# Transposes of the second half moved into the up projection, pools shared with the down projection, and other operand forms in the norms

## The chip, the cores and the metric

The kernel runs on one core of one Trainium2 chip. Its time is the device time of one execution in microseconds (us). A core has five engines, each with its own queue of instructions that it works through in order: PE (TensorE, matmuls, into PSUM), DVE (VectorE), ACT (ScalarE), POOL (GpSimd) and SP (SyncE, which here issues all DMAs). A difference of under about 0.2% (5 us) can't be told from none.

## The reference

One layer of a decoder: 2048 rows of 1024, all float32.

```python
proj = x @ w_in                       # columns: q, k, v, B, C, h, p
mix = concat(stick_breaking_attention(q, k, v), short_conv(B, C, h), multiscale_pool(p))
mix = head_group_rmsnorm(mix, mix_norm_g) @ w_o
x = layer_norm(ALPHA * x + mix, ln1_g, ln1_b)
hid = square(relu(x @ w_up))          # 4096 columns
x = layer_norm(ALPHA * x + hid @ w_down, ln2_g, ln2_b)
```

## The kernel before

Every float32 operand of a matmul is split into a high part (an ACT copy to the float32r type) and a low part (a subtraction on DVE or GpSimd), and three products (high by high, high by low, low by high) stand for one. The rows are worked on in four chunks of 512 (`c`), each of four tiles of 128 (`t`).

`phase1` has four stages, whose instructions a scheduler interleaves when the program is built: the input projections, the attention (which sets the pace of DVE), the output product with the first norm (`out_stage`), and the up projection (`Up`). A tile of rows leaves `out_stage` as `r`: PE adds up 24 products for each of two halves of 512 columns in one of two PSUM banks (`dense_ps`), DVE adds the residual (L549) and does the norm (L87 to L110), and `r` goes to memory (`x1scr`). Two products later `transposed` turns the tile: four PE transposes (128 by 128) to a bank, and from the banks seven operands `B11, T2, B21, T3, T1, T4, B22`, sums and differences of quarters for a Strassen-Winograd scheme with seven products in place of eight. `put` splits each (ACT L571, then DVE or GpSimd L572) and stores both parts in `tscr`, by way of four staging buffers.

The up projection runs over two halves of 1024 rows (chunks 0 and 1, then 2 and 3). In each, 16 `quad`s make four tiles of hidden values with seven products of 12 matmuls from the seven operands `x` (2 MB each, loaded from `tscr`) and seven weights `w` made by `weights`. The first three `x` stand in pool `upx`, the next two in `upm`, the last two and the hidden tiles `h` in `upr`. These pools take over memory of the earlier stages: `upm` that of `xw` and `mixw` (operands of the output product), `upr` that of `mixw` and `dense` (tiles `r`, staging buffers, raw loads). A tile waits until the tiles that lay there are done with. `h` goes to memory (`hscr`).

`down` opens new pools when `phase1` has closed its own. In eight groups `g` of 512 hidden columns it loads four rows of tiles of `w_down` (`draw`, split into `dh`, `dl`) and hidden values (`hr`, split into `hh`, `hl`), and makes 32 sums of 12 matmuls; DVE adds each to `y` (L832 in the first group, L834 after). In the last group each of the 16 row tiles, once complete, gets the second norm: statistics, an inverse root by ACT and three small DVE instructions (L100 to L102), the scaling on ACT (L847), the product with `ln2_g` on DVE (L848), the sum with `ln2_b` on GpSimd (L849). The last tile has a shorter path on DVE alone (L842, L843).

Of the kernel before, what the change touches and what calls it, by code (L numbers as in the profile page):

```python
# [40 lines left out]
EARLY, LATE = 4, 8  # L41


def build(nc, tc, ctx, A, out):
# [50 lines left out]
    def inverse_act(p, var):  # L95
# [22 lines left out]
    with ExitStack() as up:  # L118
        phase1(nc, tc, up, A, ident, scr, hscr, split, rsqrt, layer_norm, bcast)
    down(nc, tc, ctx, A, hscr, x1scr, lambda p, t: ln_stats(p, t, inverse_act), bcast, out)  # L120


def phase1(nc, tc, ctx, A, ident, scr, hscr, split, rsqrt, layer_norm, bcast):
# [398 lines left out]
    def out_stage(c):  # L522
# [7 lines left out]
        if c == NC - 1:  # L530
            pend.pop(0)(lambda fn: fn(), last_mix)
            att.close()
            ff.append(Up(nc, tc, ctx, A, tscr, hscr))
            with early():
                ff[0].begin(pd)
        for t in range(4):
# [22 lines left out]
            defer(lambda r=r, t=t: transposed(c, t, r), 2)  # L559

    raw = {}

    def transposed(c, t, r):

        dst, slot = tscr[c // 2], 2 * (c % 2) + t // 2

        def put(k, src, engine):
            th = pd.tile([P, NQ, P], R, name="x1h", tag="cs", bufs=4)
            tl = pd.tile([P, NQ, P], R, name="x1l", tag="cs", bufs=4)
            with early():  # L570
                nc.scalar.copy(th, src)  # L571
                engine.tensor_tensor(tl, src, th.bitcast(F), ALU.subtract)  # L572
            nc.sync.dma_start(dst[k][:, 0, slot], th.bitcast(F))
            nc.sync.dma_start(dst[k][:, 1, slot], tl.bitcast(F))

        def kept(name, tag, src):
            raw[name] = pd.tile([P, NQ, P], F, name=name, tag=tag, bufs=1)
            nc.scalar.copy(raw[name], src)

        def minus(o, a, b):  # L580
            nc.vector.tensor_tensor(o, a, b, ALU.subtract)

        for dd in range(2):
            with early():
                tp = dense_ps().rearrange("p (i t) -> p i t", i=NQ)
                for i in range(NQ):
                    d = NQ * dd + i
                    nc.tensor.transpose(out=tp[:, i, :], in_=r[:, d * P:(d + 1) * P], identity=ident)
                if t % 2 == 0:
                    kept(f"b{dd}", ("pb", "pc")[dd], tp)  # L590
                    put((B11, B21)[dd], tp, nc.vector)
                elif dd == 0:
                    kept("c0", "pa", tp)
                    minus(raw["b0"], tp, raw["b0"])
                    put(T1, raw["b0"], nc.gpsimd)
                else:
                    t2 = r[:, 0:CH].rearrange("p (i t) -> p i t", i=NQ)
                    minus(t2, tp, raw["b0"])
                    minus(raw["c0"], tp, raw["c0"])
                    put(B22, tp, nc.vector)  # L600
                    put(T2, t2, nc.gpsimd)
                    put(T3, raw["c0"], nc.gpsimd)
                    minus(raw["b1"], raw["b1"], t2)
                    put(T4, raw["b1"], nc.gpsimd)
# [30 lines left out]
    for q in quads:  # L635
        for step in q:
            pass
    ff.load(1)
    for f in range(DFF // P // 2):
        for step in ff.quad(f, 1):  # L640
            pass


class Up:
# [3 lines left out]
    def __init__(self, nc, tc, ctx, A, tscr, hscr):  # L648
        self.nc, self.tc, self.ctx, self.A, self.tscr, self.hscr = nc, tc, ctx, A, tscr, hscr
        self.px = self.pool("upx")  # L650
# [5 lines left out]

    def load(self, half, part=None):
        for i, k in enumerate(LOADS):
            if part in (None, i):
                pool = self.px if i < 3 else self.pm if i < 5 else self.pr  # L660
                t = pool.tile([P, 2, 4, NQ, P], F, name=f"x{k}")
# [3 lines left out]
    def middle(self):  # L665
        self.pm = self.pool("upm")
        for i in (3, 4):
            self.load(0, i)

    def rest(self):  # L670
        self.pr = self.pool("upr")
        for i in (5, 6):
            self.load(0, i)

    def weight(self, src):
# [3 lines left out]
        pool, bufs = (self.px, EARLY) if i < EARLY else (self.pm, LATE)  # L679
# [46 lines left out]

    def quad(self, f, half):
        nc = self.nc
        w = self.ready.pop(f) if f in self.ready and half == 0 else self.weights(self.raw(f), self.pm, 1)
# [30 lines left out]
        s = self.pm.tile([P, CH], F, name="s", tag="s", bufs=2)  # L760
# [3 lines left out]
        u2 = self.pm.tile([P, CH], F, name="u2", tag="u2", bufs=2)  # L764
# [7 lines left out]
        u3 = self.pr.tile([P, CH], F, name="u3", tag="u3", bufs=2)  # L772
# [11 lines left out]
def down(nc, tc, ctx, A, hscr, x1scr, ln_stats, bcast, out):  # L784
    pp = ctx.enter_context(tc.tile_pool(name="downps", bufs=1, space=PSUM, reuse_waits="tile"))
    pw = ctx.enter_context(tc.tile_pool(name="rows", bufs=1, reuse_waits="tile"))
# [4 lines left out]
    def rows(f):  # L791

        raw = pw.tile([P, D], F, name="draw", tag="draw", bufs=3)
# [104 lines left out]
```

## Time and profile before

| | |
|---|---|
| median of 3 runs | 2534.38 us (2533.66 to 2537.1) |
| profiled execution: its time | 2539.12 us |
| profiled execution: its span | 2537.3 us |
| mean granted TensorE clock | 0.984 |
| PE busy | 2419.0 us (95%) |
| DVE busy | 1651.0 us (65%) |
| POOL busy | 1107.5 us (44%) |
| ACT busy | 985.3 us (39%) |

Busy time counts an instruction from its start to its end; matmuls overlap, so a PE that is busy all the time can still be at either of its clock levels. Stages are best read from tables by stretch.

### The profile page before, as it was taken

To read this page: it belongs to the slowest core of one execution; us is meant where nothing else is said; L and a number is where in the kernel's file an instruction comes from. 1 tells how busy PE (TensorE), PEld (TensorE's weight loads), DVE (VectorE), ACT (ScalarE), POOL (GpSimd) and SP (SyncE) were. 2 spreads that over 40 slices of the span, in tenths; PEclk is the share of its full clock that TensorE was granted. 3 is DMA by queue.
4 is the path that set the end of the run, shared out by engine and by line. 5 is a ranking of instruction groups with operands and counts; after the bars stand their busy time and mean duration, and the time that the engine had idled before them with its cause. 6 is when DMAs were issued, how large, how long until landed. Compare 5 with 4: busy or idle time off the path is not lost. (4 is left out here: it accounts for less than half of the span.)

```text
span 2537.3 us, 32899 instructions
## 1 busy us (share of the span) xinstructions
PE 2419.0 (95%) x11728; PEld 2002.6 (79%) x11728; DVE 1651.0 (65%) x2256; ACT 985.3 (39%) x1913; POOL 1107.5 (44%) x820
## 2 busy tenths in 40 slices
PE   8999999999999999987899999999899999999996
PEld 6988888777778778765788888888688888888884
DVE  3778777878888899865565556565334443444479
ACT  4667666655665665423222223222211111111122
POOL 2557555865865865445554545454200110111033
PEclk9999999999999999999999999999999999999998
DMA  8658555532433555686533383332642221221212
GB/s 241 187 148 246 152 144 148 173 100 90 133 92 98 169 189 175 209 311 228 187 111 114 100 339 121 104 117 83 245 128 75 83 83 50 83 83 50 73 60 92
DMA packets 157940, 356.16 MB, mean 140 GB/s; under 512 B 17872, under 2 KB 34256, under 8 KB 151888
## 3 DMA queue, kind: packets, MB, share of 16 engines
q1 hardware_dynamic: 157776, 354.05, 42.8%
q8 instruction: 93, 1.52, 0.3%
q14 instruction: 71, 0.58, 0.1%
HBM read 241.00 MB, written 112.98 MB: 140 GB/s over the span
## 5 line engine op out<-in xcount | busy, mean ns | idle before, releaser
L443 POOL TENSOR_TENSOR g<-g,sig 128x512 f32<-128x512 f32 (+2 forms) x320 | 380.1, 1192 | 347.8 <-DVE g L441 159.4
L828 PE MATMUL dn<-dh,hh 128*128 128x512 f32 x1024 | 397.9, 392 | 17.9 <-ACT hh L805 11.4
L829 PE MATMUL dn<-dl,hh 128*128 128x512 f32 x1024 | 398.7, 390 | 0.0
L830 PE MATMUL dn<-dh,hl 128*128 128x512 f32 x1024 | 398.4, 390 | 0.0
L682 POOL TENSOR_TENSOR w<-raw,w 128x512 fp32r<-128x512 f32 x186 | 259.4, 1401 | 238.4 <-ACT w L681 230.7
L834 DVE TENSOR_TENSOR y<-dn,y 128x512 f32<-128x512 f32 x224 | 152.4, 687 | 298.1 <-PE dn L830 298.1
L798 POOL TENSOR_TENSOR dl<-draw,dh 128x1024 fp32r<-128x1024 f32 x32 | 81.7, 2583 | 580.5 <-ACT dh L797 580.5
L441 DVE TENSOR_TENSOR_SCAN g<-beta,g,z 128x513 f32<-128x513 f32 x192 | 244.1, 1275 | 48.5 <-ACT sig L433 46.8
L828 PEld LDWEIGHTS dn<-dh,hh 128*128 128x128 f32 x1024 | 192.8, 188 | 64.4 <-ACT hh L805 11.8
L431 ACT ACTIVATE beta<-z 128x512 f32<-128x512 f32 (+2 forms) x320 | 172.6, 540 | 166.7 <-PE z L428 152.3
L830 PEld LDWEIGHTS dn<-dh,hl 128*128 128x128 f32 x1024 | 192.4, 188 | 40.2
L829 PEld LDWEIGHTS dn<-dl,hh 128*128 128x128 f32 x1024 | 192.9, 188 | 39.2
L805 ACT CAST hh<-hr 128x512 fp32r<-128x512 f32 x128 | 69.9, 616 | 385.1 <-PE dn L829 382.7
L230 PE MATMUL dn<-xh,wh 128*128 128x512 f32 x512 | 206.9, 407 | 10.0 <-DVE qk L66 4.9
L681 ACT CAST w<-raw 128x512 fp32r<-128x512 f32 x186 | 113.3, 620 | 260.6 <-PE b L741 113.9
L428 PE MATMUL z<-k,q 128*128 128x512 f32 (+3 forms) x640 | 193.6, 382 | 19.5 <-DVE g L441 15.1
L231 PE MATMUL dn<-xl,wh 128*128 128x512 f32 x512 | 207.0, 404 | 0.0
L232 PE MATMUL dn<-xh,wl 128*128 128x512 f32 x512 | 206.9, 404 | 0.0
L464 DVE TENSOR_TENSOR tl<-tp,th 128x512 fp32r<-128x512 f32 (+1 forms) x320 | 184.3, 596 | 30.5 <-ACT th L463 29.7
L738 PE MATMUL b<-x,w 128*128 128x512 f32 x768 | 191.7, 392 | 4.7 <-DMA x<-tscr 2.4
L460 PE MATMUL tp<-ident,g 128*128 128x128 f32 x1088 | 189.6, 275 | 3.4 <-POOL g L443 2.5
L463 ACT CAST th<-tp 128x512 fp32r<-128x512 f32 (+1 forms) x320 | 160.8, 537 | 62.7 <-PE tp L460 49.5
(184 smaller groups left out, 5013.1 us busy)
## 6 DMA issues: line engine op xcount, KB each, us to landing
hscr<-h SPq DMA_DIRECT2D x128, 256.0 KB, 2.9
hr<-hscr SPq DMA_DIRECT2D x32, 1024.0 KB, 4.8
raw<-in_w_up SPq DMA_DIRECT2D x62, 512.0 KB, 4.3
x<-tscr SPq DMA_DIRECT2D x14, 2048.0 KB, 13.9
wraw<-in_w_in SPq DMA_DIRECT2D x80, 256.0 KB, 3.4
k<-kscr SPq DMA_DIRECT2D x80, 256.0 KB, 3.0
v<-vscr SPq DMA_DIRECT2D x80, 256.0 KB, 2.9
xraw<-in_xt SPq DMA_DIRECT2D x64, 256.0 KB, 3.3
```

The costliest lines, as they stand in the source:

```text
L230: nc.tensor.matmul(ps, wh, xh, start=(d == 0), stop=False)
L231: nc.tensor.matmul(ps, wh, xl, start=False, stop=False)
L232: nc.tensor.matmul(ps, wl, xh, start=False, stop=(d == ND - 1))
L428: nc.tensor.matmul(z[:, 0:w], q[:, b, j * P:(j + 1) * P], m["k"][:, 0:w], start=(b == 0), stop=(b == 1))
L441: nc.vector.tensor_tensor_scan(left, rev, idle, st["prev"][j][:, OFF - 1:OFF], ALU.mult, ALU.bypass)
L443: nc.gpsimd.tensor_tensor(gv, gv, sig[:, 0:w], ALU.mult)
L460: nc.tensor.transpose(out=tp[:, j * P:(j + 1) * P], in_=m["g"][j][:, cols], identity=ident)
L682: self.nc.gpsimd.tensor_tensor(w[:, 1], src, w.bitcast(F)[:, 0], ALU.subtract)
L738: nc.tensor.matmul(ps, wk[:, 0, d], x[:, i, :, d, :], start=(first and d == 0 and i == 0), stop=False, skip_group_check=True)
L828: nc.tensor.matmul(ps, hh[:, i, ts], dh[:, ds], start=(i == 0), stop=False)
L829: nc.tensor.matmul(ps, hh[:, i, ts], dl[:, ds], start=False, stop=False)
L830: nc.tensor.matmul(ps, hl[:, i, ts], dh[:, ds], start=False, stop=(i == 3))
```

## The change

Rows of chunks 2 and 3 are no longer turned right after their norm. The turning stands in a class `Turn`, which `out_stage` uses for chunks 0 and 1 as before; for chunks 2 and 3 `Up.turned` loads each tile again from `x1scr` and turns it after one of the quads 2 to 9 of the first half, with buffers in `upr` and two PSUM banks of its own (`turnps`). The pools `upx`, `upm` and `turnps` now live until the end of the program: `down` puts `dh`, `dl` (now `d`) and the hidden values (now `ht`) into the places of `x0` to `x4` and of four weights, loads through the four `raw` buffers of `upm`, and sums the first group in the two banks of `turnps`, the later ones in four. Late weights get six buffers for eight, `u3` one for two, and the raw weights of quad 1 are loaded ahead. In the norms, small instructions with two tensors become ones with a per-partition scalar; in the second norm the product with `ln2_g` moves to GpSimd, except for three of the last four tiles.

```diff
-EARLY, LATE = 4, 8
+EARLY, LATE = 4, 6
@@ rsqrt
+        if shape[1] == 1:
+            nc.vector.tensor_scalar(t, s, v, -0.5, ALU.mult, ALU.mult)
+            nc.vector.tensor_scalar(t, t, s, 1.5, ALU.mult, ALU.add)
+            nc.vector.tensor_scalar(s, s, t, None, ALU.mult)
+            return s
@@ inverse_act
-        nc.vector.scalar_tensor_tensor(t, var, LN_EPS, t, ALU.add, ALU.mult)
+        nc.vector.tensor_scalar(t, var, LN_EPS, t, ALU.add, ALU.mult)
         nc.vector.tensor_scalar(t, t, -0.5, 1.5, ALU.mult, ALU.add)
-        nc.vector.tensor_tensor(y, y, t, ALU.mult)
+        nc.vector.tensor_scalar(y, y, t, None, ALU.mult)
@@ out_stage
-            defer(lambda r=r, t=t: transposed(c, t, r), 2)
+            if c < 2:
+                defer(lambda r=r, t=t: turn_out.rows(c, t, [r[:, 0:CH], r[:, CH:D]]), 2)
@@ phase1
-    for q in quads:
+    turns = [(c, t) for c in (2, 3) for t in range(4)]
+    for k, q in enumerate(quads):
         for step in q:
             pass
+        if k > 1 and turns:
+            ff.turned(*turns.pop(0))
@@ Up
+    def turned(self, c, t):
+        halves = []
+        for dd in range(2):
+            r = self.pr.tile([P, CH], F, name="r", tag="r", bufs=3)
+            self.nc.sync.dma_start(r, self.x1scr[c][t][:, dd * CH:(dd + 1) * CH])
+            halves.append(r)
+        self.turn.rows(c, t, halves)
@@ down
+    def rows(g):
+        pool, tags = (pm, ("x3", "x4")) if g % 2 else (px, ("x0", "x1"))
+        dh, dl = (pool.tile([P, 4, D], R, name="d", tag=tag) for tag in tags)
...
     def hidden(g, half, j):
+        if j:
+            t = [px.tile([P, 2, CH], R, name="ht", tag="w", bufs=EARLY) for i in range(4)]
+        else:
+            whole = px.tile([P, 4, 2, CH], R, name="ht", tag="x2")
+            t = [whole[:, i] for i in range(4)]
...
-                        ps = pp.tile([P, 512], F, name="dn", tag="dn", bufs=4)
+                        pool, tag, bufs = (pp, "dn", 4) if g else (pt, "tp", 2)
+                        ps = pool.tile([P, 512], F, name="dn", tag=tag, bufs=bufs)
...
-                        nc.vector.tensor_tensor(o, o, g2, ALU.mult)
+                        late = half == 1 and j == 1 and slot > 0
+                        (nc.vector if late else nc.gpsimd).tensor_tensor(o, o, g2, ALU.mult)
```

Line numbers in these rows are those of each kernel: L787 and L790 now are L738 and L741 before, L890 to L892 are L828 to L830, L648 is L588, L691 is L662, L768 is L723, L805 is L756.

**Order, place 1.** On PE, from the end of the output product to the start of the up projection. Before, where `x_13349` is B21, `x_13570` is T3 and `x_13173`, `x_13249` are B11, T2 of the next quad:

```order
L588 MATMUL dn<-ident,r 128x128 x4
L738 MATMUL a<-x_13349,w 128x512 x8
L741 MATMUL a<-x_13349,w 128x512 x4
L588 MATMUL dn<-ident,r 128x128 x12
L738 MATMUL b<-x_13570,w 128x512 x8
L741 MATMUL b<-x_13570,w 128x512 x4
L738 MATMUL a<-x_13173,w 128x512 x8
L741 MATMUL a<-x_13173,w 128x512 x4
```

Now, with B21 as `x_13047`, T3 as `x_13331`, B11 as `x_13045` and T2 as `x_13046`, the first two rows stand there without transposes between; the last row is from quad 2, the first place where a tile is turned, some 190 matmuls after the output product:

```order
L787 MATMUL a<-x_13047,w 128x512 x8
L790 MATMUL a<-x_13047,w 128x512 x4
L787 MATMUL b<-x_13331,w 128x512 x8
L790 MATMUL b<-x_13331,w 128x512 x4
L787 MATMUL a<-x_13045,w 128x512 x8
L790 MATMUL a<-x_13045,w 128x512 x4
L787 MATMUL b<-x_13046,w 128x512 x8
...
L648 MATMUL tp<-ident,r 128x128 x8
```

The 64 transposes of chunks 2 and 3 have left the stretch between the attention and quad 2. They come later, eight at a time, between the products of quads 2 to 9.

**Order, place 2.** On SP, right behind the loads of T3, T1 and the first four raw weight tiles, now (`x_13469` is T4, `x_13471` is B22, `x1scr_3_187` the last tile of the first norm):

```order
L768 DMA raw<-in_w_up 128x1024 x4
L563 DMA x1scr_3_187<-r 128x1024
L768 DMA raw<-in_w_up 128x1024
L691 DMA x_13469<-tscr_5_193 128x4096
L691 DMA x_13471<-tscr_6_194 128x4096
L716 DMA r<-x1scr_0_180 128x512 x2
L716 DMA r<-x1scr_1_181 128x512
L805 DMA hscr_0_0_202<-h 128x512
L768 DMA raw<-in_w_up 128x1024
```

Before, fourteen stores of turned operands (`tscr`) stood between the loads of T3 and of T4; now none does, and the fifth raw tile stands ahead of T4 and B22.

**Order, place 3.** On PE, from the up to the down projection (`x_15838`/`x_15876` is T3, `x_15842`/`x_15880` T4, `x_15844`/`x_15882` B22, all of the last quad). Before:

```order
L741 MATMUL b<-x_15838,w 128x512 x4
L738 MATMUL b<-x_15842,w 128x512 x8
L741 MATMUL b<-x_15842,w 128x512 x4
L738 MATMUL c<-x_15844,w 128x512 x8
L741 MATMUL c<-x_15844,w 128x512 x4
L828 MATMUL dn<-dh,hh 128x512
```

Now:

```order
L790 MATMUL b<-x_15876,w 128x512 x4
L890 MATMUL dn<-d,ht 128x512
...
L787 MATMUL b<-x_15880,w 128x512 x8
L790 MATMUL b<-x_15880,w 128x512 x4
L892 MATMUL dn<-d,ht 128x512
L890 MATMUL dn<-d,ht 128x512
L891 MATMUL dn<-d,ht 128x512
L787 MATMUL c<-x_15882,w 128x512 x8
L790 MATMUL c<-x_15882,w 128x512 x4
L892 MATMUL dn<-d,ht 128x512 x2
```

Of the first 24 products of the down projection, 16 now stand ahead of the product with T4, three ahead of that with B22, and five behind it; on SP the first load of `o` (from `x1scr`) still stands behind the last store of `h`.

## Rows read from the trace of the kernel before

**Rows 1.** Busy time by stretch: us, then busy (instructions) by engine, PEclk, DMA share, GB/s.

```profile
860.00:1058.00 198.00, 187.65 (x978) 152.78 (x977) 189.93 (x281) 113.64 (x227) 117.97 (x93) 1.00 0.55 184
1058.00:1222.00 164.00, 127.02 (x542) 100.59 (x541) 101.07 (x153) 45.25 (x80) 75.82 (x55) 0.91 0.73 271
1222.00:1797.00 575.00, 574.11 (x2532) 475.04 (x2531) 330.39 (x391) 151.87 (x260) 276.89 (x200) 1.00 0.38 133
1797.00:1818.00 21.00, 9.61 (x36) 7.46 (x35) 6.39 (x10) 8.55 (x12) 7.56 (x4) 0.76 1.00 373
2440.00:2540.00 100.00, 74.83 (x319) 58.78 (x318) 89.58 (x158) 32.57 (x68) 36.69 (x15) 0.92 0.21 85
```

**Rows 2.** Waits of PE from 1058 to 1222: us in total, times, longest.

```profile
PE a L738 <- DVE h L751: 14.2, 1, 14.2
PE dn L516 <- DVE x1l L572: 6.9, 1, 6.9
PE dn L516 <- DVE lnv L77: 2.9, 2, 1.6
PE b L738 <- DMA x<-tscr: 2.4, 2, 2.2
PE a L738 <- ACT w L681: 2.4, 1, 2.4
PE b L738 <- ACT w L681: 1.5, 1, 1.5
```

**Rows 3.** Groups of instructions from 1058 to 1222.

```profile
L588 PE MATMUL dn<-ident,r 128*128 128x128 f32 x64 | 10.0, 278 | 4.9 <-DVE r L549 2.2 <-issue 1.9 <-DVE x1l L572 0.6
L572 POOL TENSOR_TENSOR x1l<-b,x1h 128x512 fp32r<-128x512 f32 x9 | 12.5, 1393 | 44.8 <-ACT x1h L571 44.4 <-DMA tscr<-x1l 0.4
L572 DVE TENSOR_TENSOR x1l<-dn,x1h 128x512 fp32r<-128x512 f32 x12 | 8.2, 684 | 7.5 <-DMA tscr<-x1l 7.0 <-DMA r<-in_x 0.6
L571 ACT CAST x1h<-dn 128x512 fp32r<-128x512 f32 x12 | 7.1, 588 | 13.1 <-DMA tscr<-x1h 9.3 <-DVE mv L89 3.3 <-DVE lnv L77 0.5
```

**Rows 4.** Timeline at the start of the up projection: start, us, what, [idle before].

```profile
1161.64 0.96 SPq L662 DMA_DIRECT2D x<-tscr  x2
1171.22 3.51 PE L738 MATMUL b<-x,w 128*128 128x512 f32 x8 [2.24 <-DMA x<-tscr]
1177.35 0.62 ACT L681 CAST w<-raw 128x512 fp32r<-128x512 f32 x1 [9.01 <-DMA raw<-in_w_up]
```

**Rows 5.** A small instruction of the first norm, from 850 to 1060.

```profile
L79 DVE SCALAR_TENSOR_TENSOR lnt<-lns,lnv 128x1 f32<-128x1 f32 x9 | 4.8, 530 | 0.9 <-POOL lns L78 0.9
```

**Rows 6.** Timeline and, last, a group of DMA issues: KB each, us to landing.

```profile
1809.31 0.79 PE L828 MATMUL dn<-dh,hh 128*128 128x512 f32 x1 [11.39 <-ACT hh L805]
1799.40 0.33 SPq L756 DMA_DIRECT2D hscr<-h  x1
1820.72 1.88 DVE L832 SCALAR_TENSOR_TENSOR y<-o,dn 128x512 f32<-128x512 f32 x3 [6.43 <-PE dn L830]
o<-x1scr SPq DMA_DIRECT2D x16, 512.0 KB, 3.6
```

**Rows 7.** Groups of instructions of the second norm, from 2440 on.

```profile
L849 POOL TENSOR_TENSOR o<-o,ln_b 128x1024 f32<-128x1024 f32 x15 | 36.7, 2448 | 64.8 <-DVE o L848 64.8
L848 DVE TENSOR_TENSOR o<-o,ln_g 128x1024 f32<-128x1024 f32 x15 | 20.5, 1364 | 2.9 <-ACT o L847 2.7
L100 DVE SCALAR_TENSOR_TENSOR lnt<-mv,lnt 128x1 f32<-128x1 f32 x15 | 18.7, 1249 | 0.0
L101 DVE TENSOR_SCALAR lnt<-lnt 128x1 f32<-128x1 f32 x16 | 2.3, 143 | 0.2
L806 DVE TENSOR_TENSOR hl<-hr,hh 128x512 fp32r<-128x512 f32 x8 | 5.1, 680 | 0.0
```

**Rows 8.** Timeline of the end: the last product, and DVE's last sum.

```profile
2518.07 0.39 PE L830 MATMUL dn<-dh,hl 128*128 128x512 f32 x1
2526.03 0.68 DVE L834 TENSOR_TENSOR y<-dn,y 128x512 f32<-128x512 f32 x1
```

More of the change, by code (lines that the diff above doesn't have):

```diff
@@ L1 @@
-from contextlib import ExitStack
+from contextlib import ExitStack, nullcontext
 from itertools import chain
@@ L118, in build, with phase1 @@
     with ExitStack() as up:
-        phase1(nc, tc, up, A, ident, scr, hscr, split, rsqrt, layer_norm, bcast)
-    down(nc, tc, ctx, A, hscr, x1scr, lambda p, t: ln_stats(p, t, inverse_act), bcast, out)
-def phase1(nc, tc, ctx, A, ident, scr, hscr, split, rsqrt, layer_norm, bcast):
+        pools = phase1(nc, tc, ctx, up, A, ident, scr, hscr, split, rsqrt, layer_norm, bcast)
+    down(nc, tc, ctx, A, pools, hscr, x1scr, lambda p, t: ln_stats(p, t, inverse_act), bcast, out)
+def phase1(nc, tc, whole, ctx, A, ident, scr, hscr, split, rsqrt, layer_norm, bcast):
     qscr, kscr, vscr, mscr, x1scr, tscr = scr
@@ L558, in out_stage, with bank @@
                 nc.sync.dma_start(x1scr[c][t], r)
-            defer(lambda r=r, t=t: transposed(c, t, r), 2)
[L561 to L604, printed above, removed]
+            if c < 2:
+                defer(lambda r=r, t=t: turn_out.rows(c, t, [r[:, 0:CH], r[:, CH:D]]), 2)
+    def bank():
+        with early():
+            return dense_ps()
+    turn_out = Turn(nc, tc, pd, ident, tscr, bank, {"b0": "pb", "b1": "pc", "c0": "pa", "x1h": "cs", "x1l": "cs"}, 4, early)
     for cs in ((0, 1), (2, 3)):
@@ L651, in __init__ @@
+class Up:
+    def __init__(self, nc, tc, whole, ctx, A, ident, x1scr, tscr, hscr):
+        self.nc, self.tc, self.ctx, self.A, self.ident = nc, tc, ctx, A, ident
+        self.x1scr, self.tscr, self.hscr = x1scr, tscr, hscr
+        self.whole = whole
+        self.px = whole.enter_context(tc.tile_pool(name="upx", bufs=1, reuse_waits="tile"))
+        self.first = [self.set(self.px, k) for k in LOADS[0:3]]
         self.pp = ctx.enter_context(tc.tile_pool(name="upps", bufs=1, space=PSUM, reuse_waits="tile"))
@@ L660, in load @@
                 pool = self.px if i < 3 else self.pm if i < 5 else self.pr
-                t = pool.tile([P, 2, 4, NQ, P], F, name=f"x{k}")
+                t = self.first[i] if half == 0 and i < 3 else self.set(pool, k)
                 self.nc.sync.dma_start(t, self.tscr[half][k])
@@ L665, in middle @@
     def middle(self):
-        self.pm = self.pool("upm")
+        self.pm = self.whole.enter_context(self.tc.tile_pool(name="upm", bufs=1, reuse_waits="tile"))
+        self.ps = self.pool("ups")
         for i in (3, 4):
             self.load(0, i)
+        self.ahead = self.raw(1)
     def rest(self):
@@ L673, in rest @@
             self.load(0, i)
+        pp = self.pt = self.whole.enter_context(self.tc.tile_pool(name="turnps", bufs=1, space=PSUM, side="right",
+                                                                  reuse_waits="tile"))
+        self.turn = Turn(self.nc, self.tc, self.pr, self.ident, self.tscr,
+                         lambda: pp.tile([P, CH], F, name="tp", tag="tp", bufs=2),
+                         {n: n for n in ("b0", "b1", "c0")} | {"x1h": "xs", "x1l": "xs"}, 3, nullcontext)
+    def turned(self, c, t):
[5 more added lines that the diff above has]
+        self.turn.rows(c, t, halves)
     def weight(self, src):
@@ L725, in raw, with pop_raw @@
         return raw
+    def pop_raw(self, f, half):
+        raw, self.ahead = self.ahead, None
+        return raw or self.raw(f)
     def quad(self, f, half):
         nc = self.nc
-        w = self.ready.pop(f) if f in self.ready and half == 0 else self.weights(self.raw(f), self.pm, 1)
+        w = self.ready.pop(f) if f in self.ready and half == 0 else self.weights(self.pop_raw(f, half), self.pm, 1)
         def bank(tag):
@@ L781, in quad, with down @@
         yield
-def down(nc, tc, ctx, A, hscr, x1scr, ln_stats, bcast, out):
+def down(nc, tc, ctx, A, pools, hscr, x1scr, ln_stats, bcast, out):
+    px, pm, pt = pools
     pp = ctx.enter_context(tc.tile_pool(name="downps", bufs=1, space=PSUM, reuse_waits="tile"))
-    pw = ctx.enter_context(tc.tile_pool(name="rows", bufs=1, reuse_waits="tile"))
     p = ctx.enter_context(tc.tile_pool(name="p2", bufs=1, reuse_waits="tile"))
```

101 lines of the change are left out of this document (73 added, 28 removed).

## The prediction

> **What bounds the kernel.** I read the table by stretch first [rows 1]. In the up projection (1222 to 1797) PE is busy 574 of 575 us at full clock, and the down projection up to 2440 is like it. Only less PE work or fewer PE waits can help, and the change leaves the matmuls and transposes as they are. So I looked for stretches where PE idles or runs slow. Four lie in the change's reach: the end of the attention (860 to 1058, PE idle 10.3 us, DVE busy 190 of 198), the output product with the start of the up projection (1058 to 1222), the turn to the down projection (1797 to 1818), and the end.
>
> The second is the largest. Steady PE does 2532/575 = 4.40 products of 512 columns per us. The 542 instructions of 1058 to 1222 are 64 transposes [rows 3], 12 small ones and some 466 products: 106 us of products, about 7 us of transposes (a group of four takes some 0.45 us out of the row of products, which I read off as 0.6 us of overlapping busy time less a pipeline's share) and 2 us for the small ones. That is 115 of 164 us: 49 us are lost, 37 as idle time (164 less 127.0) and 12 because the clock is at 0.91, so at the lower of its two levels (1.2 GHz for 2.4) after each long wait. The list of waits [rows 2] says for what: 14.2 us for `h`, 6.9 us for a DVE subtraction of the turning, and smaller ones.
>
> **Removing the turning from that stretch.** The 6.9 us are a product waiting for a PSUM bank that the turning holds, whose subtraction waits for a staging buffer, so for a store (7.0 us of DVE's idle time [rows 3]). The 14.2 us are quad 2 waiting for bank `a`, whose reader writes `h` in `upr`; `upr` lies where the turning's buffers lay. With the turning gone from there both causes are gone, and the transposes' own waits (4.9 us). What stays or comes:
> - waits at chunk starts and for the norm: 2.9 us today, kept at 3;
> - T3: its load is issued when the output product ends (1161.64) and ends a wait at 1171.2 [rows 4]. The product that wants it stands 34 matmuls (7.7 us) behind the output product now (order, place 1), so 9.6 less 7.7: 2 us;
> - raw weights of quad 1: cast at 1177.35, 15.7 us after the loads of T3 are issued. They are wanted after 46 matmuls (10.4 us) and the T3 wait: 3.3 us, if the loads are no faster without the stores beside them. Behind them, GpSimd has the low parts of quad 1 to make before T1's of quad 0, at 1.4 us each: 2 to 3 us more. Together 6;
> - `upr` opens when the last tile of the norm is stored. T4 and B22, with the first stores of `h` behind them, stand behind a raw load that waits for GpSimd (place 2), but are wanted only 130 and 166 matmuls (29 and 38 us) after the output product: nothing;
> - the lower clock after these waits: 12 us for 37 idle today, so 11 idle cost about 4, rounded up to 5.
> That is 16 us for 49: a gain of **33** (20 if every new wait is twice that; 41 if loads land early and the clock stays up).
>
> **The turning in the up projection.** The transposes take PE the same 7 us. New is a load of 0.25 MB for each half tile, and DVE, ACT and GpSimd get what they had before in another place: for a pair of tiles about seven instructions of 0.7 us on DVE, ten of 0.6 on ACT and four of 1.4 on GpSimd [rows 3], in 38 us. The cover is there: DVE is busy 57%, GpSimd 48%, ACT 26% [rows 1], which become some 73, 63 and 43%. What may show is order: ACT's copies wait for three staging buffers, each held until a store has landed, and weights stand behind them. Weights run ten tiles ahead of PE (twelve before), over 25 us, so I take **-3** (0 to -20).
>
> **Scalar operands.** In the first norm an instruction on 128x1 takes 530 ns in the mean [rows 5], where one with a single tensor and an immediate takes 143 (L101 [rows 7]). At the end DVE does the same arithmetic at 1249 ns (L100). Nine times 0.39 us, for up to three instructions, are 3.5 to 10 us of DVE while it sets the pace and PE idles 10.3: **+2** (0 to 5).
>
> The row suggests why: an operation with two tensors stands still while GpSimd works, and one with a single tensor does not. The Trainium skill says so (SBUF — State Buffer, Who interferes with whom): a DVE instruction with two inputs in SBUF contends with a GpSimd instruction that reads SBUF, and whoever comes second waits for the whole of the other. By that rule the same change does harm too: each row tile of the last group gives GpSimd 4.9 us in place of 2.4, and the DVE subtractions L806 have two such inputs.
>
> **Turn to the down projection.** Today 11.4 us idle, and 1.5 us at the lower clock (0.76 in rows 1): 13. Loads and splits start only when the pools are closed; now they go into tiles that are free before the last quad ends, and 19 of the first products fill the waits of its last steps (place 3). But the first group has two banks for four. After five more products PE needs a bank that DVE empties with `o`, and `o` is issued behind the last store of `h`, 1.5 us after the last product (1799.40 against 1797.92) [rows 6]. 3.6 us to land and 0.7 for L832 make 6, of which 1.1 are covered: 5 us idle, 1.5 for the clock, and 2 for first splits that come late. Gain **+5** (-1 to +11). Two banks in the rest of the first group leave DVE 2.7 us to empty one while it also splits hidden values behind GpSimd: **-2** (0 to -6).
>
> **The end.** PE waits 3.6 us for DVE after 2440, and 18.8 us pass from the last product (2518.46) to the end of the span, of which 7.5 are DVE's backlog: its last sum starts at 2526.03 [rows 8]. L848 (20.5 us) mostly leaves DVE, and L100 goes from 1249 to some 150 ns (16 us) [rows 7]. DVE then needs 3.3 of the 5.4 us that PE takes for a tile, and GpSimd 4.9 of 5.4. The backlog goes; the last tile still meets one product on DVE and one sum on GpSimd. 7 us at the end and 3 of PE's waits: **+10** (4 to 14).
>
> **Sum.** 33 - 3 + 2 + 5 - 2 + 10 = 45 us. The profiled execution took 2539.1, 4.7 more than the median; from the median the prediction is **2489 us** (2494 for an execution like the profiled one).
>
> **Rivals.**
> 1. *The turning blocks queues in the up projection.* For: 56 stores go through three staging buffers, and before, ACT waited 9.3 us for such stores in one group alone [rows 3]. Against: ten weights of lead, and 57% on DVE. At 2 to 3 us for each of eight tiles it costs 20 more: 2509.
> 2. *The gain is larger.* The loads of T3 and raw weights land early without stores beside them, the clock stays up, the first splits are in time: 8 + 6 more, 2474.
> 3. *GpSimd takes the end.* 4.9 us per tile of 5.4, and twelve L806 in the last group that stand behind it: if each waits a whole instruction (2.4 us), DVE needs 16 x 3.3 + 12 x 3.1 = 90 us for the 87 of the group, and the 10 us of the end become 2: 2497, inside the forecast's range. This is the rule above at its full price; L848 at 1364 ns against 680 for half its columns shows no such wait today.
> 4. *Slower.* SP issues in order, and the stores of turned operands now stand between the raw loads of quads 2 to 9. If every store there waits for its split, raw weights come late by some time per quad. It decides from 6 us per quad on (45/8); at 8 us: 2489 + 64 = 2553. Against: four raw buffers hold two quads (38 us).
> 5. *No change*, by a half-way of rival 4.
>
> **Chances.** The forecast (2474 to 2505) 0.62; rival 1 and like it (2505 to 2529) 0.18; larger (under 2474) 0.11; within 0.2% 0.03; slower 0.06. Rival 3 has 0.15 of the forecast's 0.62. The range for 8 in 10 leaves out 0.06 below and 0.14 above: 2468 to 2520. Faster 0.91, same 0.03, slower 0.06; 0.2% (5 us) is about what a measurement here can tell.
>
> **What would show it.** Right: no wait of 7 or 14 us between the attention and quad 2, and idle time there of some 11 us; PE at over 99% in quads 2 to 9; a wait of about 5 us for DVE after the fifth product behind the last of the up projection; 128x1 instructions under 0.25 us; some 11 us from the last product to the end. Wrong: PE waits for weights in quads 2 to 9 (rival 1 or 4), idle time from 1058 on that moved to T3 and weights and is over 20 us, or DVE still behind PE at the end.

## The result, and the profile after

The changed kernel takes **2473.4 us** (median of 4 runs, 2471.1 to 2476.9) against 2535.7 (4 runs, 2533.7 to 2538.1) of the kernel before on the same chip: a ratio of 0.9755, 95% interval 0.9738 to 0.9772, some 62 us. The forecast was 2489, in a range of 2468 to 2520. The profiled execution took 2475.4 us with a span of 2473.6, so 63.7 us less than the span of before.

Busy time by stretch in the changed kernel, columns as in [rows 1]:

```profile
850.00:1047.00 197.00, 188.53 (x972) 153.16 (x972) 187.68 (x277) 118.13 (x235) 121.79 (x96) 0.99 0.56 186
1047.00:1164.00 117.00, 110.16 (x471) 89.02 (x471) 75.53 (x132) 20.82 (x37) 44.87 (x35) 0.97 0.63 237
1164.00:1739.00 575.00, 575.00 (x2571) 476.95 (x2570) 351.77 (x416) 180.81 (x310) 316.50 (x224) 1.00 0.50 173
1739.00:1768.00 29.00, 20.16 (x87) 15.76 (x85) 15.08 (x21) 5.26 (x9) 9.87 (x4) 0.95 0.74 243
2395.00:2473.00 78.00, 66.04 (x292) 54.36 (x290) 61.61 (x129) 28.54 (x60) 59.00 (x25) 0.95 0.26 101
```

From the end of the attention to quad 2 it is 117 us in place of 164, and PE idles 6.8 us of them in place of 37. The up projection is full, with the turning in it. PE's waits in that second stretch:

```profile
PE a L787 <- ACT w L726: 3.7, 1, 3.7
PE dn L521 <- DVE r L554: 1.9, 1, 1.9
PE b L787 <- ACT w L726: 0.9, 1, 0.9
PE b L787 <- DMA x<-tscr: 0.3, 1, 0.3
```

The 14.2 and the 6.9 us of [rows 2] are gone. What is left is the wait for the raw weights of quad 1. The timeline (start, us, what, idle before it) shows why they are late:

```profile
1129.94 0.80 SPq L691 DMA_DIRECT2D x<-tscr  x2
1130.79 2.48 SPq L768 DMA_DIRECT2D raw<-in_w_up  x4
1143.97 0.62 ACT L726 CAST w<-raw 128x512 fp32r<-128x512 f32 x1 [10.64 <-DMA raw<-in_w_up]
1144.64 3.42 PE L787 MATMUL a<-x,w 128*128 128x512 f32 x8 [3.73 <-ACT w L726]
```

The loads are issued behind the 4 MB of T3 and T1, and 14.0 us pass until the first cast. Eight products after that wait take 3.42 us, where they take 1.98 at 1177.20: the granted clock from 1144.6 to 1148.1 is 0.59 in the mean, so mostly the lower of its two levels, for 1.00 at 1177.20.

At the turn to the down projection PE waits 1.3 us for first splits between its last steps of the up projection, and then one long time for the sum that needs `o`; SP issues `o` behind the last store of `h`:

```profile
1761.21 0.32 SPq L805 DMA_DIRECT2D hscr<-h  x1
1761.58 0.94 SPq L883 DMA_DIRECT2D o<-x1scr  x2
1767.11 1.29 DVE L894 SCALAR_TENSOR_TENSOR y<-o,dn 128x512 f32<-128x512 f32 x2 [5.93 <-DMA o<-x1scr]
1767.86 0.80 PE L890 MATMUL dn<-d,ht 128*128 128x512 f32 x1 [7.58 <-DVE y L894]
```

Behind that wait PE starts again at the lower of its clock levels (first row), where the kernel before is at the full clock in the same place (second row):

```profile
1767.90:1771.90 4.00, 4.00 (x10) 3.17 (x11) 0.50 (x1) 0.00 (x0) 0.00 (x0) 0.50 0.81 319
1816.20:1820.00 3.80, 3.80 (x18) 3.16 (x17) 0.00 (x0) 2.08 (x2) 2.40 (x1) 1.00 1.02 415
```

From there to the last product PE waits for nothing at all. Before, its waits from 1830 to the end were these:

```profile
PE dn L828 <- DVE y L834: 5.4, 13, 0.6
PE dn L828 <- DVE lnt L101: 1.2, 1, 1.2
```

Six of them, of some 0.49 us, stand about 12 us into the second to the seventh of the eight groups, here called group boundaries; the other eight, 3.6 us in all, in the last group. Groups of the second norm in the changed kernel, from 2395 on (busy, mean ns):

```profile
L911 POOL TENSOR_TENSOR o<-o,ln_g 128x1024 f32<-128x1024 f32 x11 | 26.7, 2428 | 8.8 <-ACT o L909 8.8
L867 DVE TENSOR_TENSOR ht<-draw,ht 128x512 fp32r<-128x512 f32 x8 | 12.6, 1600 | 0.0
L105 DVE TENSOR_SCALAR lnt<-mv,lnt 128x1 f32<-128x1 f32 x13 | 2.7, 211 | 8.2 <-ACT lnt L104 8.2
```

The first small operation is 211 ns for 1249 [rows 7], but the splits of hidden values are 1600 ns for 680: DVE's operations with two tensors now stand beside a GpSimd that is busy 59.0 of 78 us, for 36.7 of 100 before. The end, where the last product starts at 2460.66 (before, and DVE's last sum, in [rows 8]):

```profile
2462.22 0.68 DVE L896 TENSOR_TENSOR y<-dn,y 128x512 f32<-128x512 f32 x1
2464.96 2.34 POOL L912 TENSOR_TENSOR o<-o,ln_b 128x1024 f32<-128x1024 f32 x1 [2.43 <-DVE o L911]
2465.69 2.82 DVE L904 SCALAR_TENSOR_TENSOR o<-y,mv,ln_g 128x512 f32<-128x512 f32 x2 [0.69 <-DMA out<-o]
```

DVE's last sum is 1.2 us behind the last product (7.6 before), and 12.6 us pass from there to the end of the span for 18.8.

The table compares places of the timeline that all kernels here have: the end of the last product of the up projection, the row with the 25th product of the down projection, the end of the last product, and the rest of the span (us). From the changed kernel on down, 19 products of the down projection (4.3 us) already stand ahead of the first place.

| kernel | up ends | 25th product | last product | rest |
|---|---|---|---|---|
| before | 1797.9 | 1816.2 | 2518.5 | 18.8 |
| before, scalar operands | 1795.2 | 1813.2 | 2509.5 | 13.6 |
| before, product on GpSimd | 1795.6 | 1813.8 | 2514.7 | 24.5 |
| before, weights split in halves | 1793.5 | 1811.6 | 2509.4 | 18.8 |
| changed | 1759.1 | 1767.9 | 2461.0 | 12.6 |
| changed, no norm edits | 1759.1 | 1767.7 | 2464.5 | 18.9 |
| changed, turned early | 1794.5 | 1803.3 | 2497.1 | 12.8 |
| changed, product on DVE | 1757.4 | 1766.1 | 2459.3 | 14.0 |

The span's 63.7 us are thus 48.3 up to the 25th product, 9.1 from there to the last, and 6.3 behind it. Before, with the product on GpSimd, and with the weights in halves, the program is the same up to 1790, and that point still differs by 4.5 us between the three executions: the 48.3 are uncertain by 2, and 46 against the mean of the three (1813.9).

### The profile page after: what moved, and what is told of

It is laid out like the page before. It is cut to its first block, busy times and chain, and to the rows that moved or that the text cites. A ratio compares the mean times of both kernels' runs of the same rounds, so it can differ in the third digit from the quotient of the medians.

```text
span 2473.6 us, 33055 instructions
## 1 busy us (share of the span) xinstructions
PE 2406.9 (97%) x11728; PEld 2001.1 (81%) x11728; DVE 1589.4 (64%) x2243; ACT 991.1 (40%) x1913; POOL 1141.5 (46%) x833
## 4 chain that ended last, share of the span: by engine, by line
PE 82%; DVE 7%; DMA 4%; POOL 3%; issue 2%; ACT 2%; SPq 0%; DVEq 0%; ACTq 0%; POOLq 0%
PE dn L890 9%; PE dn L892 9%; PE dn L891 9%; PE b L787 7%; PE c L787 5%; PE a L787 4%; PE z L433 4%; PE dn L235 4%; PE dn L236 4%; PE dn L237 4%; PE b L790 3%; PE tp L465 3%; PE c L790 2%; PE a L790 2%; PE o L471 2%
## 5 line engine op out<-in xcount | busy, mean ns | idle before, releaser
L890 PE MATMUL dn<-d,ht 128*128 128x512 f32 x1024 | 399.2, 390 | 8.6 <-DVE y L894 7.6
L891 PE MATMUL dn<-d,ht 128*128 128x512 f32 x1024 | 399.1, 390 | 0.0
L892 PE MATMUL dn<-d,ht 128*128 128x512 f32 x1024 | 397.9, 390 | 0.3 <-DVE ht L867 0.3
L853 POOL TENSOR_TENSOR d<-draw,d 128x1024 fp32r<-128x1024 f32 x32 | 76.8, 2414 | 520.1 <-ACT d L852 511.1
L866 ACT CAST ht<-draw 128x512 fp32r<-128x512 f32 x128 | 74.5, 620 | 460.5 <-PE dn L892 443.6
L890 PEld LDWEIGHTS dn<-d,ht 128*128 128x128 f32 x1024 | 192.7, 188 | 49.4 <-DVE y L894 8.0
L892 PEld LDWEIGHTS dn<-d,ht 128*128 128x128 f32 x1024 | 192.6, 188 | 40.8 <-DVE ht L867 0.7
L891 PEld LDWEIGHTS dn<-d,ht 128*128 128x128 f32 x1024 | 192.8, 188 | 40.0
L787 PE MATMUL b<-x,w 128*128 128x512 f32 x768 | 189.6, 389 | 1.2 <-ACT w L726 0.9
```

The lines of the kernel that those rows point to most:

```text
L787: nc.tensor.matmul(ps, wk[:, 0, d], x[:, i, :, d, :], start=(first and d == 0 and i == 0), stop=False, skip_group_check=True)
L890: nc.tensor.matmul(ps, hh[:, ts], dh[:, ds], start=(i == 0), stop=False)
L891: nc.tensor.matmul(ps, hh[:, ts], dl[:, ds], start=False, stop=False)
L892: nc.tensor.matmul(ps, hl[:, ts], dh[:, ds], start=False, stop=(i == 3))
```

## The experiments

Two theories were to be told apart. A: the turning, by its stores and its memory, holds up the output product and quad 2; and DVE stands still behind GpSimd in every operation that reads two tensors from SBUF. B: the order of the loads made the gain before the up projection, and DVE's own amount of work the one at the end. Each was timed against the kernel before (whose medians were 2535.3 to 2538.4); the changed kernel's ratio to compare with is 0.9755. What was not tried alone is the six late weights for eight and the single buffer of `u3`.

**Scalar operands alone**, in the kernel before:

```diff
+        if shape[1] == 1:
+            nc.vector.tensor_scalar(t, s, v, -0.5, ALU.mult, ALU.mult)
...
-        nc.vector.scalar_tensor_tensor(t, var, LN_EPS, t, ALU.add, ALU.mult)
+        nc.vector.tensor_scalar(t, var, LN_EPS, t, ALU.add, ALU.mult)
```

> The kernel before with only the scalar operands in both norms. Theory A (a DVE operation that reads two tensors from SBUF stands still while GpSimd works, whatever its size): the first operation of the second norm falls from 1178 ns to about 210, 16 of them give 15.5 us of DVE, DVE then needs some 5.1 us of the 5.4 us that PE takes for a tile of the last group, and the backlog behind the last product goes: 10 us there and some 5 us before the up projection, about 2521 us (2517 to 2527). The six waits of 0.49 us at the group boundaries of the down projection stay. Theory B (it is the product with ln2_g on DVE that makes the backlog, the form of the small operations costs little): 5 us or less, 2531 or more.

2524.9 us, ratio 0.9949 (0.9937 to 0.9962): 13 us, theory A. From the 25th product to the last it is 696.3 us in place of 702.3, all of it in the last group, where PE's eight waits are gone; the six at the group boundaries stay. The rest is 13.6 for 18.8; GpSimd's and DVE's big operations stay:

```profile
L854 POOL TENSOR_TENSOR o<-o,ln_b 128x1024 f32<-128x1024 f32 x15 | 35.9, 2396 | 54.2 <-DVE o L853 54.2
L853 DVE TENSOR_TENSOR o<-o,ln_g 128x1024 f32<-128x1024 f32 x15 | 21.4, 1429 | 6.7 <-ACT o L852 6.7
L105 DVE TENSOR_SCALAR lnt<-mv,lnt 128x1 f32<-128x1 f32 x14 | 2.8, 201 | 0.1
```

The 5 us that were expected ahead of the up projection are not there: it ends at 1795.2, inside the spread of the unedited program.

**The product on GpSimd alone**, in the kernel before:

```diff
-                        nc.vector.tensor_tensor(o, o, g2, ALU.mult)
+                        late = half == 1 and j == 1 and slot > 0
+                        (nc.vector if late else nc.gpsimd).tensor_tensor(o, o, g2, ALU.mult)
```

> The kernel before with only the product with ln2_g on GpSimd (the last three tiles' stay on DVE). Theory A: 20 us leave DVE, but GpSimd is then busy 4.9 of 5.4 us, and the small operations with two tensors (first and last of the second norm, 1178 and 215 ns before) each wait for up to 2.4 us; the first takes about 1.9 us and the last about 1 us, so that DVE needs 5 to 6 us per tile: gain 2 to 6 us, 2530 to 2534. Theory B (the backlog is DVE's own work, which falls by 1.3 us per tile): the whole 10 us of the end, 2526, and the small operations stay at 1.2 and 0.2 us.

2540.2 us, ratio 1.0010 (1.0002 to 1.0019): no gain, if anything some 3 us slower, which is less than the 5 us that can be told from none; both expectations had a gain. Theory A's mechanism is there, at a higher price:

```profile
L100 DVE SCALAR_TENSOR_TENSOR lnt<-mv,lnt 128x1 f32<-128x1 f32 x14 | 17.5, 1251 | 4.4 <-ACT lnt L99 4.4
L102 DVE TENSOR_TENSOR lny<-lny,lnt 128x1 f32<-128x1 f32 x14 | 15.2, 1089 | 0.3
```

One number for each of 128 partitions takes 1.1 us (L102, 215 ns before). The rest behind the last product grows to 24.5 us.

**Both norm edits undone**, in the changed kernel (the two diffs above, reversed):

> The changed kernel with both edits of the norms undone: moved turning and pools alone. Theory A: the down projection's 8.9 us came in part from the pools (no subtraction of hidden values beside one of weights at the group boundaries), and the norm edits are worth what they saved before the up projection and at the end, 5 + 3.6 + 6.3: about 2489 us (2485 to 2493), with no PE wait at the group boundaries. Rival: the boundary waits were the norms' doing or follow from DVE's load: they come back, 6 us more, 2495.

2487.6 us, ratio 0.9803 (0.9790 to 0.9816): 12 to 14 us more, as theory A has it. The two profiled executions differ by 9.8 us (this one was the fastest of its five), and that lies behind the 25th product: 3.7 us up to the last product and 6.3 in the rest. The up projection ends at the same 1759.1, so no worth of the scalar operands in the first norm is to be seen. PE's waits in the down projection from 1830 on:

```profile
PE dn L885 <- DVE lnt L101: 1.2, 1, 1.2
PE dn L885 <- DVE y L891: 1.1, 3, 0.5
```

The kernel before also waits 0.49 us at each of six group boundaries there; without the norm edits they are still gone. So they left with the pools and the loads that go with them.

**Turned early**, in the changed kernel:

```diff
-            if c < 2:
-                defer(lambda r=r, t=t: turn_out.rows(c, t, [r[:, 0:CH], r[:, CH:D]]), 2)
+            defer(lambda r=r, t=t: turn_out.rows(c, t, [r[:, 0:CH], r[:, CH:D]]), 2)
...
-    turns = [(c, t) for c in (2, 3) for t in range(4)]
+    turns = []
```

> The changed kernel with the rows of chunks 2 and 3 turned where they were before, in the output stage; pools, load order and norms as changed. Theory A (the prediction's: the turning itself, its stores and the memory that it holds are what quad 2 and the output product wait for): most of the 36 us gained between the attention and quad 2 goes back, 2500 to 2510, with a long wait at quad 2's first product for h or for T4 again; the up projection is faster by the transposes' own 7 us, which are inside that number. Rival (the gain came from the load order and the raw weights fetched ahead, the turning was hidden anyway): 2473 to 2485.

2512.2 us, ratio 0.9896 (0.9883 to 0.9910): some 36 us of the gain go back, with the old waits of PE:

```profile
PE a L786 <- DVE h L799: 12.5, 1, 12.5
PE dn L521 <- DVE x1l L628: 5.8, 1, 5.8
```

The rival is out: raw weights fetched ahead and the order of loads bring little while the turning stands there. Of the 46 to 48 us ahead of the 25th product 35.4 are the turning's (1803.3 less 1767.9). Which part of them is the memory that it holds and which its stores is read from the two waits alone; no run parts the two.

**GpSimd's split of the down weights in halves**, in the kernel before:

```diff
-        nc.gpsimd.tensor_tensor(dl, raw, dh.bitcast(F), ALU.subtract)
+        for s in (slice(0, CH), slice(CH, D)):
+            nc.gpsimd.tensor_tensor(dl[:, s], raw[:, s], dh.bitcast(F)[:, s], ALU.subtract)
```

> The kernel before with GpSimd's subtraction of the down weights split in two of 128x512, the same work in shorter instructions. At each group boundary DVE's four subtractions of hidden values take 9.2 us beside four such GpSimd instructions of 2.5 us, where they take 2.5 us alone. Theory A (each DVE instruction with two tensors from SBUF waits for the end of the GpSimd instruction under way): the four take about half, 5 us, the sum behind them is in time, and the six waits of 0.49 us with their slow restart go: 6 x 0.85 = 5 us, 2530. Rival (the two share the memory's bandwidth, so both are slower as long as GpSimd works): 9 us stay, and the waits too: 2535.

2531.6 us, ratio 0.9974 (0.9965 to 0.9984): 6.6 us, theory A; 4.5 of them are in the down projection (702.3 to 697.8). A group boundary in the timeline of the kernel before:

```profile
1897.40 10.39 POOL L798 TENSOR_TENSOR dl<-draw,dh 128x1024 fp32r<-128x1024 f32 x4 [72.51 <-ACT dh L797]
1899.77 9.16 DVE L806 TENSOR_TENSOR hl<-hr,hh 128x512 fp32r<-128x512 f32 x4 [0.82 <-ACT hh L805]
1909.59 0.50 PE L828 MATMUL dn<-dh,hh 128*128 128x512 f32 x1 [0.49 <-DVE y L834]
```

and with halves, where no such wait of PE is left:

```profile
1892.71 11.88 POOL L799 TENSOR_TENSOR dl<-draw,dh 128x512 fp32r<-128x512 f32 x8 [71.85 <-ACT dh L797]
1895.09 5.84 DVE L807 TENSOR_TENSOR hl<-hr,hh 128x512 fp32r<-128x512 f32 x4 [0.82 <-ACT hh L806]
```

GpSimd works longer (11.9 us for 10.4) and DVE is done sooner (5.8 for 9.2): what DVE waits for is the end of an instruction. In the changed kernel the two no longer meet:

```profile
1874.22 2.50 DVE L867 TENSOR_TENSOR ht<-draw,ht 128x512 fp32r<-128x512 f32 x4
1880.14 4.75 POOL L853 TENSOR_TENSOR d<-draw,d 128x1024 fp32r<-128x1024 f32 x2 [73.50 <-ACT d L852]
```

**Everything turned twice** in the up projection, in the changed kernel (the second pass writes the same data):

```diff
-    turns = [(c, t) for c in (2, 3) for t in range(4)]
+    turns = [(c, t) for c in (2, 3) for t in range(4)] * 2
...
-        if k > 1 and turns:
-            ff.turned(*turns.pop(0))
+        for n in range(2):
+            if k > 1 and turns:
+                ff.turned(*turns.pop(0))
```

> The changed kernel with every tile of chunks 2 and 3 turned twice in the up projection, so that loads, transposes, splits and stores of the turning stand there in double number (16 calls in quads 2 to 9, the second pass over the same data). Theory A (the turning costs PE its transposes and nothing else: a quad with one tile takes 19.94 us, one without 19.03): 8 x 0.91 = 7.3 us more, about 2481 us, PE without waits in quads 2 to 9. Rival (its queues are near their limit, as rival 1 of the prediction has it): 2 to 3 us for each of eight tiles more, 2500 and PE waits for weights.

2488.4 us, ratio 0.9805 (0.9791 to 0.9818): 13 to 15 us, between the two. PE's waits from 1165 to 1400:

```profile
PE tp L649 <- DVE x1l L630: 5.4, 3, 2.4
PE tp L649 <- issue: 2.1, 3, 1.2
PE tp L649 <- PE b L791: 0.7, 1, 0.7
```

7.3 us of transposes (eight quads, each 0.91 us longer with one more tile) and 8.2 of waits make 15.5. The waits are the transposes' own, for splits that wait for staging buffers; none is for weights. Turning once leaves room, twice does not.

**Raw weights of quad 1 ahead of T1**, in the changed kernel:

```diff
-        for i in (3, 4):
-            self.load(0, i)
+        self.load(0, 3)
         self.ahead = self.raw(1)
+        self.load(0, 4)
```

> The changed kernel with the raw weights of quad 1 loaded ahead of T1, behind T3. In the changed kernel PE waits 3.7 us for the cast of these weights and 0.9 us more behind it, and runs some products at the lower clock. Theory A (the loads wait their turn on the DMA engines behind the 2 MB of T1): the weights land 4 us earlier, both waits go, T1 is still in time: 4 to 6 us faster than the changed kernel, 2468. Rival (the wait moves on to T1, which lands as much later): no change, 2473.

2469.2 us, ratio 0.9729 (0.9715 to 0.9742). The output product ended 2.1 us earlier in this execution (1127.06 for 1129.20), the up projection 7.0: 4.9 us are the edit's, theory A. The medians differ by 4.2 us, just under what can be told from none, so it is the trace that shows it. The 3.7 us are gone, and a wait of 1.3 is left:

```profile
1136.97 0.62 ACT L726 CAST w<-raw 128x512 fp32r<-128x512 f32 x1 [5.77 <-DMA raw<-in_w_up]
1142.86 2.14 PE L787 MATMUL b<-x,w 128*128 128x512 f32 x8 [1.32 <-ACT w L726]
```

**First two tiles of `o` early**, in the changed kernel:

```diff
-                        o = p.tile([P, D], F, name="o", tag="o", bufs=2)
-                        nc.sync.dma_start(o, x1scr[c][t])
+                        if half == j == 0 and slot < 2:
+                            o = raw([P, D], x1scr[c][t])
+                        else:
+                            o = p.tile([P, D], F, name="o", tag="o", bufs=2)
+                            nc.sync.dma_start(o, x1scr[c][t])
```

> The changed kernel with the first two row tiles of the first norm loaded into slots of the raw weights' tag, which are open before the up projection ends; the other tiles of o as before. In the changed kernel PE waits 7.6 us for the sum that empties the first of two banks, whose operand o is issued behind the last store of h. Theory A (it is the place of that load on the queue, set by the pool that opens last): the wait falls below 2 us, and the restart at the lower clock with it: 6 to 8 us faster than the changed kernel, 2466. Rival (y itself lies where the up projection's tiles lay, so the sum waits for them, or DVE is behind): 4 us or less.

2467.3 us, ratio 0.9722 (0.9709 to 0.9736). Issue of the load, and PE's wait:

```profile
1746.95 3.80 SPq L842 DMA_DIRECT2D draw<-x1scr  x2
1763.14 0.50 PE L893 MATMUL dn<-d,ht 128*128 128x512 f32 x1 [2.98 <-DVE y L897]
```

The load of `o` is issued 14.6 us earlier and the wait is 3.0 in place of 7.6; the 25th product comes 4.7 us earlier and the last 5.1. Theory A, but the wait stays above its 2 us: DVE has the last `h` of the up projection ahead of the sum (1761.81 to 1762.49).

**The product back on DVE**, in the changed kernel:

```diff
-                        late = half == 1 and j == 1 and slot > 0
-                        (nc.vector if late else nc.gpsimd).tensor_tensor(o, o, g2, ALU.mult)
+                        nc.vector.tensor_tensor(o, o, g2, ALU.mult)
```

> The changed kernel with the product with ln2_g back on DVE, scalar operands kept. Alone, the product on GpSimd made the kernel before 3 us slower, the scalar operands alone 13 us faster. Theory A (the lock: the product's move harms only while the small operations read two tensors; with scalars it is worth what it takes off the end): behind the last product 14.0 us pass, as in the kernel before with scalar operands only, for 12.6 now, so 1 to 3 us slower than the changed kernel, 2475. Rival (the two edits need each other, and the move carries a good part of the 12 us that both are worth): 2479 or more. Second rival (the move harms as before): 2470.

2474.4 us, ratio 0.9757 (0.9741 to 0.9773): no difference that can be measured. The rest is 14.0 us for 12.6, as expected, and the product's move is worth that at most.

**Both earlier loads**, the raw weights of quad 1 ahead of T1 and the first two tiles of `o` early together:

> The changed kernel with both earlier loads: raw weights of quad 1 ahead of T1, and the first two tiles of o in slots of the raw weights. Theory A (the two waits lie 600 us apart and have nothing to do with each other): the sum of the two single gains, 4 + 6 us, 2463 (2459 to 2465); by the ratios to the kernel before, 0.970. Rival (what one gains the other loses, as the up projection takes the gain up): 2467.

**2461.7 us**, ratio 0.9712 (0.9694 to 0.9730): by the medians the sum of the two gains (4.2 and 6.1 us), by the ratios somewhat less. In the trace PE's two waits are 1.3 and 3.0 us, as short as in the single runs. This is faster than both kernels, by some 11 us against the changed one.

**The end edited**, on top of that:

```diff
-                        late = half == 1 and j == 1 and slot > 0
+                        late = half == 1 and j == 1 and slot > 1
                         (nc.vector if late else nc.gpsimd).tensor_tensor(o, o, g2, ALU.mult)
-                        nc.gpsimd.tensor_tensor(o, o, b2, ALU.add)
+                        for ds in (slice(0, 512), slice(512, D)) if late else (slice(0, D),):
+                            nc.gpsimd.tensor_tensor(o[:, ds], o[:, ds], b2[:, ds], ALU.add)
```

> The same with the end edited: of the last four tiles the second's product goes to GpSimd too, and the third's sum with ln2_b is made on GpSimd in two halves. In the changed kernel that second product takes 1.9 us on DVE just before the last products end, and DVE's first operation of the last tile (two tensors) takes 2.1 us for 0.7 behind GpSimd's 2.3 us sum. Theory A (DVE waits for the end of the GpSimd instruction under way): 1 to 2 us less from the last product to the end, 2461. Rival (GpSimd, with 4.8 us more in the last 15, now ends last): no gain, 2463 or more.

2463.6 us, ratio 0.9716 (0.9700 to 0.9731): nothing gained. The last tile's first operation did fall from 3.2 to 2.0 us, but it started 1.6 us after DVE's instruction ahead of it.

**And with four output tiles** for the last four row tiles:

```diff
-                    o = p.tile([P, D], F, name="o", tag="o", bufs=2)
+                    pool, tag, bufs = (pm, "raw", 4) if half == j == 1 else (p, "o", 2)
+                    o = pool.tile([P, D], F, name="o", tag=tag, bufs=bufs)
```

> The kernel with both earlier loads and the edited end, and the output tiles of the last four row tiles in slots of the raw weights' tag (four, free by then) in place of two of their own. With the edited end alone the first operation of the last tile took 2.0 us for 3.2, but started 1.6 us after the DVE instruction ahead of it, and 12.8 us passed from the last product to the end, as before the edit. Theory A (it waited for a store out of one of two output tiles): it starts at once, and some 11 us pass; the median, whose spread is of that size, 2460 to 2462. Rival (GpSimd's later sum holds the end): 12.5 us or more.

2461.8 us, ratio 0.9713 (0.9697 to 0.9728), with 12.7 us behind the last product. Theory A was right that it would start at once, and wrong on the gain; the rival's number came, not by its cause:

```profile
2452.28 2.34 POOL L917 TENSOR_TENSOR o<-o,ln_b 128x1024 f32<-128x1024 f32 x1
2453.10 2.60 DVE L915 TENSOR_TENSOR o<-o,ln_g 128x1024 f32<-128x1024 f32 x1
2455.78 2.93 POOL L917 TENSOR_TENSOR o<-o,ln_b 128x512 f32<-128x512 f32 x2 [1.16 <-DVE o L915]
2455.86 3.40 DVE L908 SCALAR_TENSOR_TENSOR o<-y,mv,ln_g 128x512 f32<-128x512 f32 x2
```

Starting earlier, DVE's two operations ran into GpSimd's two: 2.60 us for some 1.2, 3.40 for 1.4. In these rows it is GpSimd's sums of the two tiles before the last that keep the end at some 12.6 us; no run moved them elsewhere.

## Why the prediction came out as it did

The sign, the order of the terms and the range were right; the sum of 45 us was 17 too small. The measured 2473.4 lies just below the forecast's own band (2474 to 2505), in the one called larger, which had a chance of 0.11. By its terms:

- **The stretch before the up projection (+33).** The causes named are the right ones: the waits for `h` and for the staging buffer left with the turning and came back with it (turned early). From the attention's end to quad 2 there are now 459 products, 104 us, and about 1.5 us of small ones in 117: 11 us lost for the 49 of before and the 16 expected, so about 38 gained. T3 came almost in time (0.3 for 2), T1's low part cost nothing (2 to 3 in the sum), and the waits at chunk starts were 1.9 for 3, the lower clock some 4 for 5. The raw weights were late as predicted, 4.6 us for 3.3.
- **Turning in the up projection (-3).** It costs PE its transposes and no wait: 575.0 of 575 us busy. Doubling it shows what the term was afraid of, 8 us of waits, so the margin is real but smaller than a factor of two.
- **Scalar operands in the first norm (+2).** None to be seen: with and without them the up projection ends at 1759.1. With them the attention's last product comes earlier (1047.2 for 1052.7), but PE reaches the end of the output product no sooner (1129.2 for 1129.1).
- **Turn to the down projection (+5) and two banks (-2).** Together right, and partly by luck. 18.3 us from the last product of the up projection to the 25th became 8.8, and 4.3 of the difference were work done ahead: 5.2. But the 25th product is where PE starts again: it and the eleven behind it take 4.8 us at the lower clock, where twelve take 2.7 before, so 2.1 go back and 3.1 are left, for the 3 of the two terms. The place of the wait was right (behind `o`, after the last store), its length 7.6 us for 5; two banks cost nothing, as every later twelve products of the group take 2.7 us.
- **The down projection itself.** Here is the step that failed: it had nothing for PE's waits up to the last group, and 3 us for those in it. A group is 384 products, 87.0 us without a wait. Before, each of the six groups between the first and the last takes 87.8 us, and the last 93.4; in the changed kernel these seven take 87.0 to 87.2. That is 4.8 us for nothing and 6.2 for 3; with the 2.1 of the restart off, it is the 9.1 of the table up to 0.2. A wait costs more than its length even at the full clock: 0.49 us cost 0.8, and the eight of the last group, 3.6 us in all, cost 6.2. I took L806 at the 680 ns of the last group [rows 7], where GpSimd has no weights to split, and not over the whole stage, and read "PE is like the up projection" from busy time. Six boundaries, each with 0.49 us of wait and a slow restart, were there to be read. They are gone since GpSimd's four subtractions no longer lie beside DVE's four; halves showed the same gain in the kernel before. In the last group the scalar operands alone, in the kernel before, bring the whole 6.2; the pools without the norm edits bring 2.2 of it.
- **The end (+10).** 6.3 us behind the last product for 7, and the 6.2 above for 3: near enough, but for another reason than stated. It was put down to the product and the scalar operands together. The scalar operands make nearly all of it alone (13.6 us behind the last product, 696.3 ahead); the product alone makes it worse, and with scalars its move is worth 1.4 us in the trace and nothing in the median.

About 5 of the 63.7 us are not settled. Most of them lie ahead of the end of the attention, where executions of the same program differ by up to 4 us, and the execution of before that the prediction reads was the longest of three.

Of the rivals, the second's 2474 is the number that came, but mostly by another way: the raw weights were cast hardly earlier than before (14.0 us after the issue of T3 for 15.7), and the first splits came late by 1.3 us for 2. T3 in time and a clock of 0.97 bear it out in part; a part as large was the down projection, which it did not name. The first holds only when the turning is doubled. The third describes what GpSimd does to L867 correctly (1600 ns for 680), without taking the end, because DVE has room there once the small operations are free. The fourth and fifth did not show: no product in quads 2 to 9 waits for weights.

## What to carry to other kernels

Before GpSimd is given elementwise work, look at what DVE runs beside it: here an operation with two tensors from SBUF, be it on one number for each of 128 partitions, waited for the end of GpSimd's instruction, and one with a tensor and a scalar operand did not. A wait of half a microsecond that comes once per group is worth reading over a whole stage, and the mean duration of an operation is taken from the place where it matters, not from the stage's end. Work whose result is wanted late goes into a stage where PE is the bound and the others have room, and what PE waits for after that may be no more than a load's place in the queue, which is cheap to move (4.9 and 5.1 us here).

## What the runs showed of the hardware

Four DVE subtractions of 128x512 take 2.5 us alone, 9.2 beside four GpSimd subtractions of 128x1024, and 5.8 beside eight of 128x512: so DVE does not run slower, it waits for the end of an instruction. The Trainium skill has this as its rule (SBUF — State Buffer, Who interferes with whom: the port pair that the two share is an exclusive lock, and a DVE instruction with two inputs in SBUF contends for it with a GpSimd instruction that reads SBUF); these runs agree. They add what it costs on one number per partition: 1.1 to 1.25 us per operation beside GpSimd at its busiest, 0.2 us with a scalar operand in its place. An operation with two tensors of which one lies in PSUM did not wait either: beside the same busy GpSimd in the changed kernel's last group, DVE's sums of a bank and `y` stay at 0.67 us.

```profile
L896 DVE TENSOR_TENSOR y<-dn,y 128x512 f32<-128x512 f32 x25 | 16.7, 669 | 2.3 <-PE dn L892 2.3
```
